# Fewer chunks for layer 1's queries and gates, planned buffer counts, and the last weighting shared by three engines

## The chip, the cores and the metric

The kernel runs on one core of a Trainium2 chip. The metric is the device time of one execution in microseconds (us). The engines are named as the profile names them: PE (TensorE, matmul), PEld (its weight load), DVE (VectorE), ACT (ScalarE), POOL (GpSimd) and SP (SyncE, which here issues transfers). A name with q behind it (ACTq, SPq) is that engine's sequencer, where transfers and waits on semaphores stand.

## The reference

Two layers work on 1040 tokens (16 meta tokens and 1024 real ones) of width 1024. The meta tokens fall away at the end, and a last RMS norm is applied.

```python
for layer in range(2):
    u = rms_norm(h, norm_g[layer])
    dq, dk, dv, dz, fq, fk, fv, fz, f_logit = split(u @ w_in[layer])
    # 4 "diff" heads: two rotated query/key pairs of 64 each, values of 128
    q1, q2 = rope(dq parts); k1, k2 = rope(dk parts)
    p = softmax(causal(q1 k1^T / 8)) - lam * softmax(causal(q2 k2^T / 8))
    o_a = rms_norm(p @ v_a, subln_g) * (1 - lambda_init)
    # 8 "fox" heads of 64: softmax with a cumulative forget bias, no rope
    p = softmax(causal(q_f k_f^T / 8 + cum_q - cum_k))
    o_b = p @ v_f
    h = h + concat(o_a * silu(dz), o_b * silu(fz)) @ w_out[layer]
return rms_norm(h, final_g)[16:]
```

## The kernel before

Every fp32 operand of a large matmul is split into a high and a low part, and a product of two such operands is three matmuls: high by high, low by high, high by low. The transposed, normed activations lie in SBUF as `XTh` and `XTl` (1024 channels as 8 groups of 128, by 1040 tokens). A projection of 128 output columns is `proj` (L344): for each chunk of tokens, 8 channel groups times 3 matmuls into one PSUM tile `pj`, as wide as the chunk. The chunks of a projection come from a list: layer 0 uses `CH_ALL`, or `CH_BLK` where the chunks have to end on token blocks. Layer 1's queries and gates are needed for the 1024 real tokens alone and use `CH_REAL` (L334), three chunks of 342, 342 and 340 columns. All keys use the full 1040 tokens in both layers.

A layer has eight units: 0 to 3 are the diff heads, 4 to 7 are pairs of fox heads. A unit is its projections of keys and queries (`unit_proj`, L482; the values of units 0 and 1 come from `proj_v01`, L384 to L423, whose matmul is L417), its attention (`attend`, L834), and its gate (`unit_gate`, L646). A layer ends with the out projection (matmul L1073), and per block of 128 tokens `out_half` (L1096 adds, L1097 squares) for each half of 512 channels and `out_close` (L1099).

For a diff unit, a chunk that PE has finished is copied by ACT (L502, tile `raw`), swapped by four transfers into `sw`, multiplied by cosine on DVE (L511) and by sine on POOL (L512), added on DVE (L513), and split into a high and a low part on ACT (L526) and DVE (L519). These steps run over groups of chunks: `RCH` is 2, so the three chunks of a query make a group of 684 columns and one of 340. Queries lie in the tiles `qa0`, `qa1` and `ql`, keys in `k0` and `k1`; a transfer on ACTq (L141) copies the high part to the other 64 partitions. Then come the scores (PE L690, L692, and L810, L811 for the meta tokens), the softmax on DVE (L696), ACT (L703) and POOL (L720), the transposes of the probabilities (PE L855, L865, L879), their split (ACT L773, DVE L774), and the products with the values (PE L795 to L800, L777 for the meta keys).

The program text doesn't fix the order on the engines. A scheduler with a planner's timeline (L1182) orders the instructions, and it also chooses how many buffers a tag has, wherever the kernel gives no number. `STB` = 3 gives a number to the tags `k0`, `k1`, `qa0`, `qa1` and `ql`. These tags hold more than keys and queries: at the start, the input blocks `hb` and the normed blocks `u` stand in them, and so does the raw weight of the first queries (`wraw4`, L306); at each layer's end, the split out weights `wo_k`, `wo_qa`, `wo_ql` do.

At the very end, `out_close` of the last token block works out the factor `r` of the norm on DVE, and then, for each half, `rms_apply` (L271) multiplies by `r` and by the gain `gb` in one DVE instruction, and SP issues the transfer out.

Of the kernel before, what the change touches and what calls it, by code (L numbers as in the profile page):

```python
# [16 lines left out]
AF = mybir.ActivationFunctionType  # L17
# [3 lines left out]
NM = 16  # L21
# [27 lines left out]
ENG = ('g','d')  # L49
WLB = 6  # L50
VPB = 0
STB = 3
NQZ = 3
PMB = 4
OTB = 2
# [58 lines left out]
def hybrid_kernel(ctx: ExitStack, tc: tile.TileContext, x, meta, norm_g, w_in, b_forget,  # L114
# [50 lines left out]

    small = [("es", 4, 272), ("ck", 2, 384), ("subn", 2, 36), ("sst", SSB, 8), ("ss", 3, 16), ("fn", 1, 64), ("fm", 1, 8), ("wf", 1, 64)]
    cst = const.tile([P, P + 96 + MW // 2 + sum(n * w for _, n, w in small)], F32, name="cst")
    rings, at = {}, P + 96 + MW // 2  # L170
    for nm, n, w in small:
# [159 lines left out]
        return his, los  # L331

    CH_ALL = [(0, 348), (348, 346), (694, 346)]
    CH_REAL = [(NM, 342), (NM + 342, 342), (NM + 684, 340)]  # L334
    CH_BLK = [(0, NM + 2 * P), (NM + 2 * P, 3 * P), (NM + 5 * P, 3 * P)]

    late = []
# [659 lines left out]
    for l in range(DEPTH):  # L997
# [101 lines left out]
        def out_close(opened):  # L1099

            b, hb, u, ss = opened
            t0, n = blk(b)
            if l == 0 and b > 0:
                dma(h1[t0:t0 + n], hb[:n])
            v, r = ss[:, 1, 0:1], ss[:, 2, 0:1]
            nc.vector.tensor_scalar(out=v[:n], in0=ss[:n, 0, 0:1], scalar1=1.0 / D, scalar2=EPS,
                                    op0=ALU.mult, op1=ALU.add)
            nc.vector.scalar_tensor_tensor(out=v[:n], in0=ss[:n, 0, 1:2], scalar=1.0 / D, in1=v[:n],
                                           op0=ALU.mult, op1=ALU.add)
            rsqrt(ss[:, 2], ss[:, 1], n, 1, ss[:, 3])  # L1110
            if l == 0:
                rms_apply(hb, n, r, gb, u)
                return lambda: put_ut(b, u)
            for hf in range(2):
                c = slice(512 * hf, 512 * hf + 512)
                rms_apply(hb[:, c], n, r, gb[:, c], u[:, c])
                dma(out2[P * (b - 1):P * b, c], u[:, c])
            return lambda: None

# [66 lines left out]
```

## Time and profile before

| what | value |
|---|---|
| median of 3 runs (lowest, highest) | 1485.57 us (1485.4, 1487.66) |
| the profiled execution's own time, its span | 1487.34 us, 1485.6 us |
| TensorE clock granted over the span | 0.983 of full |
| PE busy | 1416.9 us, 95% of the span |
| DVE, ACT, POOL busy | 958.7, 698.6, 619.2 us |
| chain of waits that ended last: PE, DVE, DMA | 75%, 7%, 4% of the span |

A busy share is the time in which an engine had an instruction running. The chain of waits follows the last instruction back, step by step, to what released it; its shares say which engine's work filled the time.

### The profile page before, as it was taken

What the parts mean: (1) busy time and instruction counts of PE and PEld (TensorE: products, weight loads), DVE (VectorE), ACT (ScalarE), POOL (GpSimd) and SP (SyncE); (2) the same over time, 40 slices, a digit from 0 to 9 for tenths busy, and PEclk for the clock granted to TensorE, in tenths of its full rate; (3) what the DMA queues carried; (4) which work ended last, traced back from release to release, by engine and by line L of the source; (5) the groups of instructions that cost most, each with busy time, mean ns of one, the idle gap of its engine ahead of it and who ended that gap; (6) DMA issues with size and microseconds to landing.
All of it is one profiled execution on the core that took longest, in us unless ns stands there. A gap on an engine that the chain in (4) does not pass through costs nothing.

```text
span 1485.6 us, 26706 instructions
## 1 busy us (share of the span) xinstructions
PE 1416.9 (95%) x9262; PEld 1350.0 (91%) x9262; DVE 958.7 (65%) x2721; ACT 698.6 (47%) x1729; POOL 619.2 (42%) x1118
## 2 busy tenths in 40 slices
PE   4889989999999999999998989999999999999997
PEld 4888989999999999996888989899999999999886
DVE  4548796867765666655654678677757565655554
ACT  3335554545554555554323455444446455544511
POOL 2616463542435443654015345445424444445400
PEclk7999999999999999999999999999999999999999
DMA  9315240353324234358333142324331323253632
GB/s 193 74 30 73 39 93 16 65 62 69 71 49 71 61 56 82 82 152 200 114 110 75 29 60 48 68 47 64 53 87 29 82 44 80 55 118 91 228 109 91
DMA packets 112215, 119.63 MB, mean 81 GB/s; under 512 B 15376, under 2 KB 92816, under 8 KB 112080
## 3 DMA queue, kind: packets, MB, share of 16 engines
q1 hardware_dynamic: 104592, 104.09, 32.2%
q10 hardware_dynamic: 7488, 13.83, 4.7%
q8 instruction: 73, 1.20, 0.3%
q14 instruction: 62, 0.51, 0.1%
HBM read 70.92 MB, written 21.54 MB: 62 GB/s over the span
## 4 chain that ended last, share of the span: by engine, by line
PE 75%; DVE 7%; DMA 4%; ACT 2%; issue 2%; SPq 1%; POOL 1%; DVEq 0%; ACTq 0%; POOLq 0%
PE pj L352 36%; PE pss L1073 5%; PE pj L1073 5%; PE pss L690 4%; PE pss L692 4%; PE pt L865 4%; PE po L800 3%; PE pj L417 3%; PE po L799 2%; DMA sw<-raw 1%; SPq L137 1%; DVE E L696 1%; PE pt L1073 1%; DVE raw L511 1%; DMA mt<-ms 1%
## 5 line engine op out<-in xcount | busy, mean ns | idle before, releaser
L352 PE MATMUL pj<-XTh,whi 128*128 128x346 f32 (+5 forms) x1392 | 453.8, 328 | 5.0 <-ACT XTh L296 1.9
L352 PE MATMUL pj<-XTh,wlo 128*128 128x346 f32 (+5 forms) x1392 | 452.9, 326 | 1.2 <-POOL wlo L328 1.2
L352 PE MATMUL pj<-XTl,whi 128*128 128x346 f32 (+5 forms) x1392 | 451.8, 325 | 1.1 <-DVE XTl L297 1.1
L352 PEld LDWEIGHTS pj<-XTh,whi 128*128 128x128 f32 x1392 | 264.3, 190 | 9.0 <-POOL whi L325 1.9
L352 PEld LDWEIGHTS pj<-XTh,wlo 128*128 128x128 f32 x1392 | 265.1, 190 | 2.5 <-POOL wlo L328 1.8
L352 PEld LDWEIGHTS pj<-XTl,whi 128*128 128x128 f32 x1392 | 264.8, 190 | 2.3 <-DVE XTl L297 1.7
L696 DVE CUSTOM_DVE_ANT_0 E<-pss,cst 128x346 f32<-128x346 f32 (+6 forms) x384 | 212.0, 558 | 77.0 <-PE pss L692 61.7
L703 ACT ACTIVATE E<-E,cst 128x656 f32<-128x656 f32 (+3 forms) x192 | 172.5, 898 | 141.7 <-DVE cst L696 137.8
L328 POOL TENSOR_TENSOR wlo<-wraw,whi 128x256 fp32r<-128x256 f32 x232 | 182.1, 785 | 16.3 <-PE pt L760 1.3
L774 DVE TENSOR_TENSOR ptl<-pt,pth 128x512 fp32r<-128x512 f32 (+1 forms) x240 | 147.6, 633 | 34.8 <-ACT pth L773 30.7
L690 PE MATMUL pss<-k,qa 128*128 128x400 f32 (+7 forms) x448 | 152.8, 347 | 12.1 <-DVE cst L696 6.9
L773 ACT CAST pth<-pt 128x512 fp32r<-128x512 f32 (+1 forms) x240 | 123.3, 545 | 72.8 <-PE pt L865 30.9
L325 POOL TENSOR_SCALAR whi<-wraw 128x256 fp32r<-128x256 f32 x232 | 101.0, 436 | 116.4 <-DMA wraw<-in_w_in_dram 115.2
L720 POOL TENSOR_SCALAR E<-E,cst 128x400 f32<-128x400 f32 (+2 forms) x96 | 83.7, 873 | 138.2 <-DVE cst L719 127.2
L673 POOL TENSOR_SCALAR XTl<-ql 64x128 fp32r<-64x128 f32 x136 | 53.0, 396 | 151.3 <-PE pss L692 127.3
L690 PEld LDWEIGHTS pss<-k,qa 128*128 128x128 f32 x448 | 84.8, 190 | 16.9 <-DVE cst L696 9.7
L865 PE MATMUL pt<-cst,E 128*128 128x128 f32 x576 | 87.1, 273 | 0.3 <-DVE cst L762 0.3
L799 PE MATMUL po<-pth,V 128*128 128x256 f32 x320 | 82.7, 283 | 0.0
L800 PE MATMUL po<-ptl,V 128*128 128x256 f32 x320 | 82.3, 286 | 0.0
L512 POOL TENSOR_TENSOR sw<-sw,sin 128x694 f32<-128x694 f32 (+5 forms) x32 | 50.6, 1581 | 76.0 <-DMA sw<-raw 63.8
L692 PE MATMUL pss<-k,q 68*128 68x400 f32 (+6 forms) x224 | 71.7, 326 | 0.5 <-DMA qa<-qa 0.5
L692 PE MATMUL pss<-k,XTl 128*128 128x400 f32 (+6 forms) x224 | 71.5, 325 | 0.0
(303 smaller groups left out, 2944.3 us busy)
## 6 DMA issues: line engine op xcount, KB each, us to landing
wraw<-in_w_in_dram SPq DMA_DIRECT2D x244, 128.0 KB
hb<-in_x_dram SPq DMA_DIRECT2D x16, 512.0 KB
wor<-in_w_out_dram SPq DMA_DIRECT2D x64, 128.0 KB
ms<-OT SPq DMA_DIRECT2D x8, 520.0 KB
k<-k ACTq DMA_DIRECT2D x16, 260.0 KB
h<-hb SPq DMA_DIRECT2D x8, 512.0 KB
ms<-OT SPq DMA_DIRECT2D x8, 512.0 KB
hb<-h SPq DMA_DIRECT2D x8, 512.0 KB
```

The lines of the kernel that those rows point to most:

```text
L328: nc.gpsimd.tensor_tensor(out=lo, in0=raw, in1=hi.bitcast(F32), op=ALU.subtract)
L352: nc.tensor.matmul(ps[:, :n], lhsT=w, rhs=xx[:, k, t0:t0 + n], start=(cnt == 0), stop=(cnt == 23))
L690: nc.tensor.matmul(ps[:, :nn], lhsT=U.Qa[m][:, t:t + P], rhs=U.K1[m][:, c0:c0 + nn], start=True, stop=False)
L692: nc.tensor.matmul(ps[:, :nn], lhsT=low[m], rhs=U.Kb[m][:, c0:c0 + nn], start=False, stop=True)
L696: nc.vector.tensor_tensor_reduce(out=E[:, c0:c0 + n], in0=ps[:, :n], in1=k, scale=-1.0, scalar=s[:, c - 1:c] if CHN and c else -NEG, op0=A ...
L703: nc.scalar.activation(E[:, :W], E[:, :W], AF.Exp, scale=-1.0, bias=lo, accum_out=s[:, 4:5])
L773: nc.scalar.copy(hi, ps)
L774: nc.vector.tensor_tensor(out=lo, in0=ps, in1=hi.bitcast(F32), op=ALU.subtract)
L799: nc.tensor.matmul(o[:, :256], lhsT=U.V[:, kb, hd, :], rhs=hi, start=False, stop=False)
L800: nc.tensor.matmul(o[:, :256], lhsT=U.V[:, kb, hd, :], rhs=lo, start=False, stop=last)
L865: nc.tensor.transpose(ps[:, (2 * a + b) * P:(2 * a + b + 1) * P], PP[:, k0:k0 + P], ident)
L1073: nc.tensor.matmul(ps, lhsT=xx[:, k, m0:m0 + P], rhs=wo[k][w][:, c], start=(k == 0 and i == 0), stop=(k == KT - 1 and i == 2))
```

## The change

There are four edits. `CH_REAL` becomes two chunks of 512 columns, for 16 projections of layer 1; with `RCH` = 2, both chunks of a query now make one group of 1024 columns. The ring `ck` in SBUF has slots of 512 instead of 384 columns, since a chunk of a fox query now needs them. `STB` becomes 0, so that the planner chooses the number of buffers for `k0`, `k1`, `qa0`, `qa1` and `ql`: it takes 2 of each. It also chooses anew for the tags that it planned before: the PSUM tag `pj` gets 3 instead of 2, `pss` 4 instead of 3; the others keep their numbers. And in the last block, half 0 is multiplied by the gain on POOL as soon as its sum is there (tile `hg`), and by `r` on ACT (L1118 of the changed kernel), while DVE does half 1.

```diff
--- before.py
+++ after.py
@@ -49,7 +49,7 @@
 ENG = ('g','d')
 WLB = 6
 VPB = 0
-STB = 3
+STB = 0
 NQZ = 3
 PMB = 4
 OTB = 2
@@ -165,7 +165,7 @@
 
 
 
-    small = [("es", 4, 272), ("ck", 2, 384), ("subn", 2, 36), ("sst", SSB, 8), ("ss", 3, 16), ("fn", 1, 64), ("fm", 1, 8), ("wf", 1, 64)]
+    small = [("es", 4, 272), ("ck", 2, 512), ("subn", 2, 36), ("sst", SSB, 8), ("ss", 3, 16), ("fn", 1, 64), ("fm", 1, 8), ("wf", 1, 64)]
     cst = const.tile([P, P + 96 + MW // 2 + sum(n * w for _, n, w in small)], F32, name="cst")
     rings, at = {}, P + 96 + MW // 2
     for nm, n, w in small:
@@ -331,7 +331,7 @@
         return his, los
 
     CH_ALL = [(0, 348), (348, 346), (694, 346)]
-    CH_REAL = [(NM, 342), (NM + 342, 342), (NM + 684, 340)]
+    CH_REAL = [(NM, 512), (NM + 512, 512)]
     CH_BLK = [(0, NM + 2 * P), (NM + 2 * P, 3 * P), (NM + 5 * P, 3 * P)]
 
     late = []
@@ -1113,7 +1113,11 @@
                 return lambda: put_ut(b, u)
             for hf in range(2):
                 c = slice(512 * hf, 512 * hf + 512)
-                rms_apply(hb[:, c], n, r, gb[:, c], u[:, c])
+                if b == NB and hf == 0:
+
+                    nc.scalar.activation(u[:, c], hg, AF.Copy, scale=r)
+                else:
+                    rms_apply(hb[:, c], n, r, gb[:, c], u[:, c])
                 dma(out2[P * (b - 1):P * b, c], u[:, c])
             return lambda: None
 
@@ -1127,6 +1131,7 @@
                 for hf in range(2):
                     out_mm(acc[b][hf], b, hf, k)
         todo = []
+        hg = None
         for b in first:
             ob = out_open(b)
             for hf in range(2):
@@ -1141,6 +1146,9 @@
                 for k in range(KT):
                     out_mm(ps2[hf], b, hf, k)
                 out_half(ob, ps2[hf], hf)
+                if l == 1 and b == NB and hf == 0:
+                    hg = st("hg")[:, :512]
+                    nc.gpsimd.tensor_tensor(out=hg, in0=ob[1][:, 0:512], in1=gb[:, 0:512], op=ALU.mult)
             for f in todo:
                 f()
             todo = [out_close(ob)]
```

PE has 384 matmuls fewer, DVE 33 instructions, ACT 26, POOL 11.

The order on the engines changes over the whole program, since the planner works with other counts. Three places show it. First, DVE at the start, where L271 makes the normed blocks: `u_242` to `u_244` are blocks 3 to 5, `u_304` to `u_306` are blocks 6 to 8, and L297 splits a transposed block. Before:

```order
L271 SCALAR_TENSOR_TENSOR u_242<-hb_167,cst_87,gb_142 128x1024
L271 SCALAR_TENSOR_TENSOR u_243<-hb_169,cst_87,gb_142 128x1024
L271 SCALAR_TENSOR_TENSOR u_244<-hb_171,cst_87,gb_142 128x1024
...
L271 SCALAR_TENSOR_TENSOR u_304<-hb_173,cst_87,gb_142 128x1024
L271 SCALAR_TENSOR_TENSOR u_305<-hb_175,cst_87,gb_142 128x1024
L271 SCALAR_TENSOR_TENSOR u_306<-hb_177,cst_87,gb_142 128x1024
L297 TENSOR_TENSOR XTl_97<-pt_260,XTh_96 128x4x128
```

After:

```order
L271 SCALAR_TENSOR_TENSOR u_304<-hb_173,cst_87,gb_142 128x1024
L271 SCALAR_TENSOR_TENSOR u_305<-hb_175,cst_87,gb_142 128x1024
L248 SCALAR_TENSOR_TENSOR cst_87<-cst_87 128x3
L271 SCALAR_TENSOR_TENSOR u_306<-hb_177,cst_87,gb_142 128x1024
...
L271 SCALAR_TENSOR_TENSOR u_242<-hb_167,cst_87,gb_142 128x1024
L271 SCALAR_TENSOR_TENSOR u_243<-hb_169,cst_87,gb_142 128x1024
L271 SCALAR_TENSOR_TENSOR u_244<-hb_171,cst_87,gb_142 128x1024
...
L297 TENSOR_TENSOR XTl_97<-pt_260,XTh_96 128x4x128
```

Blocks 6 to 8 are now normed ahead of blocks 3 to 5. On PE, the transposes keep the order of the blocks, 3 first.

Second, PE at the first scores of layer 0. L417 makes the values of units 0 and 1, 24 matmuls for each block of tokens (one name `pj_1024_...` each); L810 and what follows are scores. Before, they stand behind the second block of tokens, and one pair of L690 and L692 follows:

```order
L417 MATMUL pj_1024_703<-vwh,XTl 128x264
L810 MATMUL pss<-k_423,qa_527 128x16
L811 MATMUL pss<-k_423,XTl 128x16
L810 MATMUL pss<-k_424,qa_528 128x16
L811 MATMUL pss<-k_424,XTl 128x16
L690 MATMUL pss<-k_423,qa_527 128x400
L692 MATMUL pss<-k_423,XTl 128x400
L417 MATMUL pj_1024_733<-vwh,XTh 128x264
```

After:

```order
L417 MATMUL pj_1024_733<-vwh,XTl 128x264
L810 MATMUL pss<-k_423,qa_527 128x16
L811 MATMUL pss<-k_423,XTl 128x16
L810 MATMUL pss<-k_424,qa_528 128x16
L811 MATMUL pss<-k_424,XTl 128x16
L690 MATMUL pss<-k_423,qa_527 128x400
L692 MATMUL pss<-k_423,XTl 128x400
L690 MATMUL pss<-k_424,qa_528 128x400
L692 MATMUL pss<-k_424,XTl 128x400
L417 MATMUL pj_1024_763<-vwh,XTh 128x264
```

They now stand behind the third block's 24 matmuls, and two pairs of L690 and L692 stand there. In layer 1 the first scores moved likewise, from behind 48 of the matmuls of L417 to behind 96.

Third, DVE at the end of layer 1's attention. L789, L774 and L769 belong to attention, L1041 and L1053 to the out projection's operands (weights and gated outputs), L659 to a gate. Before:

```order
L789 TENSOR_TENSOR pm<-pt,pm 32x256
L774 TENSOR_TENSOR ptl<-pt,pth 128x512 x3
L659 SCALAR_TENSOR_TENSOR cst<-cst,pj_3840_17142 128x342
L774 TENSOR_TENSOR ptl<-pt,pth 128x384
L769 TENSOR_TENSOR OT<-po,otmp 64x256
L659 SCALAR_TENSOR_TENSOR cst<-cst,pj_3840_17170 128x340
L1053 TENSOR_TENSOR XTl<-mt,XTh 128x384 x3
L1041 TENSOR_TENSOR wo_k_17309<-wor,wo_k_17308 128x256 x2
L659 SCALAR_TENSOR_TENSOR cst<-cst,pj_3968_17223 128x342
L659 SCALAR_TENSOR_TENSOR cst<-cst,pj_3968_17251 128x342
L1041 TENSOR_TENSOR wo_k_17309<-wor,wo_k_17308 128x256 x2
L1053 TENSOR_TENSOR XTl<-mt,XTh 128x640 x2
```

After:

```order
L769 TENSOR_TENSOR OT<-po,otmp 64x256
L789 TENSOR_TENSOR pm<-pt,pm 32x256
L774 TENSOR_TENSOR ptl<-pt,pth 128x512 x2
...
L1053 TENSOR_TENSOR XTl<-mt,XTh 128x384
L1053 TENSOR_TENSOR XTl<-mt,XTh 128x640
L1041 TENSOR_TENSOR wo_ql<-wor,wo_qa_16884 128x256 x4
L774 TENSOR_TENSOR ptl<-pt,pth 128x512
L774 TENSOR_TENSOR ptl<-pt,pth 128x384
L1041 TENSOR_TENSOR wo_e<-wor,wo_e 128x256 x4
L769 TENSOR_TENSOR OT<-po,otmp 64x256
L1053 TENSOR_TENSOR XTl<-OT,XTh 128x640
```

The last attention's steps now stand among those of the out projection. On PE it is the same: before, no matmul of an out projection (L1073) stood ahead of its layer's last product with the values (L800), in either layer; now 83 rows of L1073 in layer 0 and 61 in layer 1 do.

How many matmuls stand on PE between the last one of a unit's query projection and the unit's first score, by the order:

| unit | 0 | 1 | 2 | 3 | 4 | 5 | 6 | 7 |
|---|---|---|---|---|---|---|---|---|
| layer 0 before | 68 | 142 | 144 | 141 | 97 | 118 | 99 | 117 |
| layer 0 after | 92 | 172 | 258 | 247 | 230 | 497 | 306 | 414 |
| layer 1 before | 64 | 42 | 70 | 64 | 32 | 43 | 94 | 76 |
| layer 1 after | 112 | 92 | 215 | 220 | 176 | 333 | 281 | 239 |

## Rows read from the trace of the kernel before

**Rows 1.** The page, part 1: busy us, share of span, instructions.

```profile
PE 1416.9 (95%) x9262; PEld 1350.0 (91%) x9262; DVE 958.7 (65%) x2721; ACT 698.6 (47%) x1729; POOL 619.2 (42%) x1118
```

**Rows 2.** Windows by stage: width, busy us (instructions) by engine, granted clock, DMA.

```profile
0.00:50.00 50.00, 25.48 (x146) 23.83 (x147) 25.21 (x66) 19.64 (x38) 21.85 (x44) 0.76 0.84 166
75.00:300.00 225.00, 209.12 (x1418) 200.98 (x1417) 170.24 (x486) 112.12 (x290) 105.32 (x185) 0.98 0.30 53
300.00:675.00 375.00, 374.99 (x2596) 367.46 (x2595) 245.18 (x739) 197.58 (x502) 168.81 (x327) 1.00 0.39 79
800.00:880.00 80.00, 70.49 (x477) 68.00 (x476) 57.16 (x158) 38.49 (x96) 30.84 (x55) 0.96 0.31 50
880.00:1040.00 160.00, 152.30 (x1031) 148.17 (x1030) 121.02 (x341) 79.47 (x198) 75.20 (x134) 0.98 0.29 53
```

**Rows 3.** Waits of PE: line, what for; total us, times, longest us.

```profile
PE pss L690 <- DVE cst L696: 6.9, 7, 2.0
PE po L777 <- DVE pm L789: 6.0, 4, 2.8
```

**Rows 4.** Timeline of PE, 342 columns in layer 1: start us, duration us, instruction.

```profile
1080.69 0.32 PE L352 MATMUL pj<-XTh,whi 128*128 128x342 f32 x1
...
1083.36 0.33 PE L352 MATMUL pj<-XTl,whi 128*128 128x342 f32 x1
```

**Rows 5.** Timeline of PE, 512 columns in the last out projection.

```profile
1473.82 0.39 PE L1073 MATMUL pss<-wo_ql,XTl 128*128 128x512 f32 x1
...
1475.45 0.40 PE L1073 MATMUL pss<-wo_ot,XTh 128*128 128x512 f32 x1
```

**Rows 6.** Timeline of PE, first scores of layer 0.

```profile
79.78 0.25 PE L810 MATMUL pss<-k,qa 128*128 128x16 f32 x1 [3.89 <-ACT V L421]
```

**Rows 7.** Timelines of PE, SPq, POOL, DVE, ACT, first scores of layer 1.

```profile
796.12 0.32 PE L352 MATMUL pj<-XTl,wroom 128*128 128x340 f32 x1
...
808.08 0.67 PE L690 MATMUL pss<-k,qa 128*128 128x400 f32 x1 [3.85 <-DMA qa<-qa]
796.16 4.95 SPq L137 DMA_DIRECT2D sw<-raw  x8
800.29 2.36 POOL L512 TENSOR_TENSOR sw<-sw,sin 128x684 f32<-128x684 f32 x1 [1.38 <-DMA sw<-raw]
803.71 0.87 DVE L513 TENSOR_TENSOR raw<-raw,sw 128x684 f32<-128x684 f32 x1
804.67 0.76 ACT L526 CAST qa<-raw 64x684 fp32r<-64x684 f32 x1 [1.93 <-DVE raw L513]
```

**Rows 8.** Timelines of DVE and PE, the start.

```profile
33.17 3.67 DVE L271 SCALAR_TENSOR_TENSOR u<-hb,cst,gb 128x1024 f32<-128x1024 f32 x3
...
38.43 3.81 DVE L271 SCALAR_TENSOR_TENSOR u<-hb,cst,gb 128x1024 f32<-128x1024 f32 x3
42.90 0.33 PE L286 MATMUL pt<-cst,u 128*128 128x128 f32 x1 [3.44 <-DVE XTl L297]
```

**Rows 9.** Timelines of DVE and ACT at the end; SP's transfers out (ns min/median/max).

```profile
1477.74 0.69 DVE L1096 TENSOR_TENSOR hb<-pss,hb 128x512 f32<-128x512 f32 x1 [3.89 <-PE pss L1073]
...
1481.00 1.42 DVE L271 SCALAR_TENSOR_TENSOR u<-hb,cst,gb 128x512 f32<-128x512 f32 x2
1478.46 0.63 ACT L1097 ACTIVATE u<-hb 128x512 f32<-128x512 f32 x1 [4.81 <-DVE hb L1096]
L137 SPq DMA_DIRECT2D out_dram<-u x16: 332/333/463, 1427.1 to 1482.4; - x16
```

**Rows 10.** Timelines of POOL and DVE, two rotary products that start together.

```profile
264.02 1.69 POOL L512 TENSOR_TENSOR sw<-sw,sin 128x694 f32<-128x694 f32 x1 [3.62 <-ACT sq L742]
264.19 2.25 DVE L511 TENSOR_TENSOR raw<-raw,cos 128x694 f32<-128x694 f32 x1
...
995.81 0.88 DVE L511 TENSOR_TENSOR raw<-raw,cos 128x694 f32<-128x694 f32 x1 [0.61 <-DMA sw<-raw]
995.85 2.38 POOL L512 TENSOR_TENSOR sw<-sw,sin 128x694 f32<-128x694 f32 x1 [10.91 <-DMA sw<-raw]
```

## The prediction

> **What bounds the kernel now.** I read the page's busy times first. PE is busy for 1416.9 of 1485.6 us, DVE for 958.7, ACT and POOL for less [rows 1]. So a gain comes from less matmul time, or from the 5% in which PE has nothing to do, or from what stands after PE's last matmul.
>
> Then I asked the windows where the 5% lie. From 300 to 675 us, the fox units, PE idles 0.01 us of 375 at full clock. From 75 to 300 us, the diff units of layer 0, it idles 225 − 209.1 = 15.9 us, and the granted clock is 0.98, which costs 0.02 × 225 = 4.5 more: 20.4. From 800 to 880 us it is 9.5 + 0.04 × 80 = 12.7, and from 880 to 1040 us 7.7 + 0.02 × 160 = 10.9. Together 44.0 us are lost in the diff units of the two layers. The first 50 us idle 24.5 [rows 2]. The reader is to see two kinds of stage: fox units, where PE is fed all the time and only fewer matmuls help, and diff units, where the order of the work decides.
>
> Next come the waits that end PE's idle time in the diff units. The longest two are 3.89 us ahead of the first scores of layer 0, put down to the values' copy on ACT [rows 6], and 3.85 us ahead of those of layer 1, for the transfer of the split queries [rows 7]. Waits for DVE's softmax and for the meta probabilities are 6.9 + 6.0 = 12.9 us over eleven places [rows 3].
>
> **Fewer chunks.** Twenty 342-column matmuls lie between 1080.69 and 1083.36 us with 17 steps between the two: 0.157 us each [rows 4]. Seven steps of 512 columns lie between 1473.82 and 1475.45: 0.233 each [rows 5]. A projection takes 24 × 3 × 0.157 = 11.3 us in three chunks (the 340 wide one, two columns less, makes it 0.04 less), and 24 × 2 × 0.233 = 11.2 in two. That is 0.08 a projection, and 1.3 for 16, all on PE and so on the path: **−1.3**. It is a small edit: the columns stay, and 384 matmuls go. DVE's and ACT's fewer instructions lie under PE and are worth nothing by themselves.
>
> **The last weighting.** After the last matmul, DVE adds (1477.74), ACT squares, DVE works out the factor, and two L271 take 1.42 us from 1481.00 [rows 9]. Now ACT does half 0 while DVE does half 1. The nearest row for ACT is its square of the same 128x512 at 0.63 us, so both halves are done after about 0.71, half of the 1.42. Both transfers then want SP at once, and the second waits for the first's issue, 0.33 by the median of sixteen [rows 9]: 0.71 − 0.33 makes **−0.4**, between 0 and −0.7. POOL's product with the gain has no row; L512's 694 columns took 1.69 alone, so 512 take about 1.25. It starts after the add of half 0, and DVE then sits idle for 3.89 us before 1477.74 [rows 9], with 3.3 more to 1481.0, so POOL's product is hidden. Without that cover it would cost up to 1.25.
>
> Here a shared port matters. Where POOL's L512 started first, at 264.02, it took 1.69 us, and DVE's L511, 0.17 later, 2.25; where DVE was first, at 995.81, DVE took 0.88 and POOL 2.38 [rows 10]. The first one keeps its speed and the other pays for both. That is the rule of the Trainium skill, "SBUF — State Buffer", section "SBUF: two separate sides": the port pair that DVE and GpSimd share is an exclusive lock, taken by whichever starts first, when the DVE operation has two SBUF inputs and the GpSimd one reads SBUF. The rule speaks against giving POOL a share of DVE's work: had its product run beside L271, the gain of 0.4 would turn to a loss of about 0.5 (1.25 less 0.71). The 3.89 us of idle DVE keep the two apart, so the sum is not changed.
>
> **The first scores.** In layer 0, 24 more value matmuls stand ahead of them. What PE waited for, 3.89 us, is mostly the same work done earlier or later, so the wait itself goes if 24 matmuls are enough. Those of L417 are 264 wide; from the 342 wide, an estimate is 264/342 × 0.157 = 0.121 each, so 24 are 2.9 us. Bounds 0 and −3.9; I take **−2.9**.
>
> In layer 1 the queries now come as one group of 1024 columns. Before, the query ended at 796.4, and the group of 684 was swapped from 796.16, when its buffer came free. Now: copy 0.6 (estimate), four issues at 0.6, landing 1.7 (796.16 + 2.4 to 800.29), POOL 2.36 × 1024/684 = 3.5, add 0.87 × 1.5 = 1.3, two casts 2 × 0.76 × 1.5 = 2.3, transfer and wait 1.9 (from 806.2, where the casts end, to 808.08). From 796.4 this ends at 810.1 [rows 7]. Before, 64 matmuls and 3.85 us of waiting filled the 11.7 us to 808.08; 48 more at 0.121 fill until about 796.4 + 7.8 + 5.8 = 810.0. The longer chain and the longer cover meet: I take **−3.5**, bounds 0 (the values' copies, which now stand on ACT ahead of the casts, hold it) and −3.9.
>
> **The other diff units.** The order puts 172 to 258 matmuls between query and scores where 142 to 144 stood in layer 0, and 92 to 220 where 42 to 70 stood in layer 1. Of the 44.0 us lost there, 7.7 are the two first waits and 12.9 are softmax and meta waits, which come from DVE's own pace. That leaves 23.4, waits for the chains of keys and queries and matmuls at half clock after a wait. More cover helps these; buffers reduced from three to two hold some back. I take two fifths, **−9**, between 0 and −23; the fraction is a choice, and the largest uncertainty.
>
> **What it costs.** At the start, blocks 3 to 5 are normed after blocks 6 to 8. Their L271 end at 38.43 + 3.81 = 42.2 instead of 33.17 + 3.67 = 36.8, and PE wants block 3 first: 5.4 us late, of which the 3.44 us that PE waited at 42.90 anyway may be got back [rows 8]. I take **+3**, between 2 and 5.4. At each layer's end, attention now stands within the out projection. What was run ahead as cover is no longer there to fill the last units' softmax; out-projection matmuls have to, and their weights wait for the buffers of the last keys and queries. Before, no wait of that kind is in the trace, so bounds are 0 and, if the last unit runs as the stretch 800 to 880 does now, 12.7 each. I take **+3** in layer 0 and **+2** in layer 1.
>
> **Sum.** −1.3 − 0.4 − 2.9 − 3.5 − 9 + 3 + 3 + 2 = −9.1. The profiled execution took 1487.34 us, with a span of 1485.6; it would be 1478.2. The median of the runs is 1.8 below that execution: 1485.57 − 9.1, about 1476.
>
> **The rivals.** First, stalls only move. The diff units' DVE is busy for 170.2 of 225 us already, and with softmax as the pace, each wait that goes is given back at the next. Then −9 and −2.9 fall away, the start and the ends stay, and −1.3 − 0.4 − 3.5 + 8 gives +2.8: about 1488; with start and ends at half of their 8, 1484. For it speak the 12.9 us for DVE; against it, that fox units follow, where PE never waits.
>
> Second, slower: the ends of the layers starve. Everything ahead goes as forecast, but the last units lack fillers, and each end loses the 12.7 us of the stretch 800 to 880. That is 25.4 instead of 5: 1476 + 20 = 1496. It decides from 15 us at the two ends together. Against it speaks that out-projection matmuls are many and depend on no one softmax; for it, that their operands (L1053, L1041) are made on the same DVE as the softmax.
>
> Third, the cover ends nearly all of the 23.4 us, and the ends cost nothing: 1476 − 14 − 5 = 1457.
>
> **How the numbers follow.** Forecast 0.45, from 1468 to 1482 by itself; first rival 0.23; second 0.2; third 0.12. A measurement of this kernel can tell about 0.2% or 3 us from no change. Faster than 1482.6: the forecast, the third rival, and little of the first: 0.6. Within: 0.18, most of the first. Slower than 1488.5: 0.22, the second and the upper part of the first. The range reaches into the second and third: 1461 to 1494.
>
> **What would show it.** In the changed profile: no wait over 1 us ahead of L810 at about 80 us or of L690 at about 810; from 75 to 300 and 800 to 1040 us, PE idle of about 22 in place of 33.1; the transposes L286 waiting for L271 near 38 to 42 us; waits of L1073, L799 or L690 within the out projections of under 3 us each; DVE with one L271 at the end. Wrong would make it: new waits of L690 for the 1024-wide query chain, DVE waits of over 7 us at a layer's end, or waits of L352 for the weight splits on POOL.

## The result: slower by 0.7%

Ten runs of the changed kernel have a median of 1499.45 us (1494.13 to 1504.21), ten of the kernel before 1489.24 us (1483.5 to 1493.53). The ratio is 1.007, with a 95% interval from 1.0047 to 1.0093. The median of the three runs that stood ahead of the prediction, 1485.57 us, is 3.7 us under the median of all ten; on its scale the result is 1485.57 × 1.007 = 1496.0. The profiled execution took 1500.85 us with a span of 1499.1, so the two profiled executions are 1500.85 − 1487.34 = 13.5 us apart.

The page's busy times and its chain by engine, of the changed kernel:

```profile
PE 1424.7 (95%) x8878; PEld 1317.0 (88%) x8878; DVE 957.5 (64%) x2688; ACT 695.4 (46%) x1702; POOL 618.4 (41%) x1107
PE 79%; DMA 6%; DVE 6%; issue 3%; POOL 3%; ACT 2%; SPq 1%; ACTq 0%; DVEq 0%; POOLq 0%
```

PE is busy for a little longer, 1424.7 instead of 1416.9 us [rows 1], though it has 384 matmuls fewer. The waits of PE (us in total, times, longest) say where it stood still:

```profile
PE pt L286 <- DVE u L271: 20.0, 3, 16.1
PE pj L1068 <- POOL wo_ot L1041: 4.2, 1, 4.2
PE po L777 <- DVE pm L789: 3.9, 4, 2.6
PE pss L690 <- DVE cst L696: 3.8, 4, 2.8
PE pss L690 <- DMA qa<-qa: 2.9, 1, 2.9
```

The 3.89 us ahead of layer 0's first scores [rows 6] are gone; the waits for softmax and meta probabilities are 3.8 and 3.9 instead of 6.9 and 6.0 [rows 3], and 2.8 of the 3.8 is one wait at the end of layer 0. New is a wait of 4.2 us in the out projection.

Where the time went is read best by the steps of the program. I cut each trace at four events: the first score; the first product with the values of a fox unit (L800); layer 1's first value matmul (L417); layer 1's first product of a fox unit. For each stage I summed how much later each matmul started than the columns of the one before it need; one that started sooner counts against the sum. That need is 0.457 ns a column, from [rows 4, 5], and at least 0.11 us, the step of the 128 column transposes (L865) where nothing holds them. This loss takes in waits and slow clock together. The windows of the changed kernel at these events (columns as in [rows 2]):

```profile
0.00:82.00 82.00, 55.99 (x349) 54.56 (x349) 44.46 (x92) 31.06 (x63) 41.70 (x66) 0.83 0.62 129
82.00:426.00 344.00, 330.50 (x2208) 317.42 (x2207) 237.57 (x701) 160.72 (x425) 146.97 (x268) 0.99 0.34 57
426.00:821.00 395.00, 381.86 (x2357) 348.61 (x2357) 237.83 (x675) 182.69 (x453) 157.40 (x284) 0.99 0.40 93
821.00:1156.00 335.00, 322.12 (x2014) 298.46 (x2013) 230.30 (x628) 157.09 (x376) 142.04 (x259) 0.98 0.36 58
1156.00:1414.00 258.00, 257.07 (x1629) 236.05 (x1628) 171.23 (x481) 149.00 (x349) 121.99 (x223) 1.00 0.39 93
```

From 426 to 821 us, layer 0's fox units and its end, PE idles 395 − 381.9 = 13.1 us. In the kernel before, PE idled 0.01 us from 300 to 675 [rows 2], and 1.9 in the whole stage, from 398 to 798. The loss by stage, in us:

| stage | before | changed | difference |
|---|---|---|---|
| start, to the first score | 34.3 | 33.1 | −1.2 |
| diff units of layer 0 | 22.0 | 26.8 | +4.8 |
| fox units and end of layer 0 | 4.8 | 23.7 | +18.9 |
| diff units of layer 1 | 28.6 | 20.5 | −8.1 |
| fox units and end of layer 1 | 3.4 | 2.3 | −1.1 |
| sum | 93.1 | 106.4 | +13.3 |

So the gain in layer 1's diff units is there, and layer 0 eats it, in a stage that was nearly without loss. By the same count, some 16.6 of layer 0's 23.7 us fall between 650 and 725 us, its end, where the kernel before loses 1.8; the fox units ahead of it lose some 7 instead of 3. At the end of layer 0, PE shows this:

```profile
669.67 0.75 PE L690 MATMUL pss<-k,qa 128*128 128x456 f32 x1 [2.79 <-DVE cst L696]
...
680.67 0.50 PE L1073 MATMUL pss<-wo_qa,XTh 128*128 128x512 f32 x1 [1.20 <-POOL wo_qa L1041]
...
717.32 0.66 PE L1068 MATMUL pj<-wo_ot,mm 128*48 128x512 f32 x1 [4.20 <-POOL wo_ot L1041]
```

The wait of 2.79 us is for DVE, whose rows ahead of it are these:

```profile
665.38 0.54 DVE L696 CUSTOM_DVE_ANT_0 E<-pss,cst 128x328 f32<-128x328 f32 x1
665.86 0.08 DVE L696 DVE_READ_ACCUMULATOR2_ANT cst<- 128x1 f32 x1
665.86 1.30 DVE L1053 TENSOR_TENSOR XTl<-mt,XTh 128x400 fp32r<-128x400 f32 x2
667.08 0.41 DVE L1041 TENSOR_TENSOR wo_k<-wor,wo_ql 128x256 fp32r<-128x256 f32 x1
668.55 0.58 DVE L1053 TENSOR_TENSOR XTl<-mt,XTh 128x400 fp32r<-128x400 f32 x1 [1.06 <-ACT XTh L1052]
669.04 0.56 DVE L696 CUSTOM_DVE_ANT_0 E<-pss,cst 128x392 f32<-128x392 f32 x1
```

Between two steps of the softmax (L696) stand three splits of gated outputs and one of an out weight (L1053, L1041), and the third of the former waited 1.06 us for ACT. The softmax went on 3.1 us after the step before it had ended, and PE waited for it: here it is the order on DVE that costs.

POOL shows this:

```profile
708.25 0.41 POOL L325 TENSOR_SCALAR whi<-wraw 128x256 fp32r<-128x256 f32 x1 [3.94 <-DMA wraw<-in_w_in_dram]
...
709.43 0.80 POOL L661 TENSOR_TENSOR OT<-OT,cst 128x346 f32<-128x346 f32 x1
714.46 0.40 POOL L325 TENSOR_SCALAR whi<-wraw 128x256 fp32r<-128x256 f32 x1 [4.23 <-DMA wraw<-in_w_in_dram]
715.87 0.72 POOL L1041 TENSOR_TENSOR wo_ot<-wor,wo_ot 128x256 fp32r<-128x256 f32 x1 [1.00 <-DMA ms<-OT]
```

The wait of 4.20 us is for `wo_ot`, an out weight that POOL splits (L1041). Its buffer is the one in which the last unit's gated output stood, and POOL did that product (L661) only at 709.43, behind a split of layer 1's weights (L325) that had waited 3.94 us for its transfer. The last row of attention's output in that buffer (DVE L769, 705.73 to 706.16) had been ready 3.3 us before. Behind the product came the transfer of the output (`ms<-OT`), issued at 710.26, and L1041 waited until that had landed and began at 715.87. A second such split at 714.46 had waited 4.23 us, but was done before that. Around the two waits, the windows 667 to 681 and 712 to 725 us show the idle time and the clock:

```profile
667.00:681.00 14.00, 9.12 (x31) 6.90 (x32) 11.44 (x32) 10.38 (x26) 5.48 (x8) 0.76 0.84 248
712.00:725.00 13.00, 8.80 (x32) 5.89 (x31) 1.64 (x2) 0.58 (x1) 5.03 (x8) 0.87 0.69 86
```

In the first, PE idles 4.9 of 14 us, and the granted clock is 0.76; in the second it idles 4.2 of 13, at 0.87. So for part of the time the matmuls behind the waits run at the lower of the clock's two levels (1.2 GHz), which is worth 0.24 × 14 + 0.13 × 13 = 5.1 us. With the idle time that is 14.2 of the 16.6 us of layer 0's end. In the kernel before, layer 0's attention was over when its out projection began.

### The profile page after: what moved, and what is told of

Same layout as the page of the kernel before. It is cut to its first block, busy times and chain, and to the rows that moved or that the text cites. A ratio compares the mean times of both kernels' runs of the same rounds, so it can differ in the third digit from the quotient of the medians.

```text
span 1499.1 us, 25917 instructions
## 1 busy us (share of the span) xinstructions
PE 1424.7 (95%) x8878; PEld 1317.0 (88%) x8878; DVE 957.5 (64%) x2688; ACT 695.4 (46%) x1702; POOL 618.4 (41%) x1107
## 3 DMA queue, kind: packets, MB, share of 16 engines
q1 hardware_dynamic: 103824, 104.09, 33.1%
## 4 chain that ended last, share of the span: by engine, by line
PE 79%; DMA 6%; DVE 6%; issue 3%; POOL 3%; ACT 2%; SPq 1%; ACTq 0%; DVEq 0%; POOLq 0%
PE pj L352 39%; PE pss L1073 5%; PE pj L1073 5%; PE pss L690 4%; PE pss L692 4%; PE pt L865 3%; DMA wraw<-in_w_in_dram 3%; PE pj L417 2%; PE po L799 2%; PE po L800 2%; PE po L797 1%; PE po L795 1%; PE po L796 1%; DVE E L696 1%; PE pt L1073 1%
## 5 line engine op out<-in xcount | busy, mean ns | idle before, releaser
L352 PE MATMUL pj<-XTh,whi 128*128 128x346 f32 (+4 forms) x1272 | 433.5, 343 | 14.0 <-POOL whi L325 3.2
L352 PE MATMUL pj<-XTh,wlo 128*128 128x346 f32 (+4 forms) x1272 | 432.7, 341 | 0.9 <-POOL wlo L328 0.8
L352 PE MATMUL pj<-XTl,whi 128*128 128x346 f32 (+4 forms) x1272 | 431.5, 340 | 0.9 <-DVE XTl L297 0.9
L352 PEld LDWEIGHTS pj<-XTh,whi 128*128 128x128 f32 x1272 | 241.1, 190 | 28.4 <-POOL whi L325 3.7
L696 DVE CUSTOM_DVE_ANT_0 E<-pss,cst 128x456 f32<-128x456 f32 (+6 forms) x384 | 211.9, 558 | 70.9 <-PE pss L692 42.4
L352 PEld LDWEIGHTS pj<-XTh,wlo 128*128 128x128 f32 x1272 | 242.3, 191 | 10.6 <-POOL wlo L328 2.2
L352 PEld LDWEIGHTS pj<-XTl,whi 128*128 128x128 f32 x1272 | 242.0, 190 | 10.2 <-DVE XTl L297 1.1
L703 ACT ACTIVATE E<-E,cst 128x400 f32<-128x400 f32 (+2 forms) x192 | 172.4, 898 | 141.8 <-DVE cst L696 135.9
L328 POOL TENSOR_TENSOR wlo<-wraw,whi 128x256 fp32r<-128x256 f32 x232 | 177.1, 764 | 52.1 <-PE pj L352 38.1
L325 POOL TENSOR_SCALAR whi<-wraw 128x256 fp32r<-128x256 f32 x232 | 104.6, 451 | 227.6 <-DMA wraw<-in_w_in_dram 169.3
L774 DVE TENSOR_TENSOR ptl<-pt,pth 128x512 fp32r<-128x512 f32 (+1 forms) x240 | 148.3, 633 | 51.2 <-ACT pth L773 40.4
L690 PE MATMUL pss<-k,qa 128*128 128x400 f32 (+7 forms) x448 | 151.1, 341 | 8.1 <-DVE cst L696 3.8
L690 PEld LDWEIGHTS pss<-k,qa 128*128 128x128 f32 x448 | 85.0, 190 | 14.7 <-DVE cst L696 5.9
L865 PE MATMUL pt<-cst,E 128*128 128x128 f32 x576 | 83.6, 273 | 1.4 <-DVE cst L762 1.2
L800 PE MATMUL po<-ptl,V 128*128 128x256 f32 x320 | 83.0, 288 | 0.5 <-POOL ptl L885 0.5
L692 PE MATMUL pss<-k,q 68*128 68x400 f32 (+6 forms) x224 | 72.8, 328 | 0.0
L865 PEld LDWEIGHTS pt<-cst,E 128*128 128x128 f32 x576 | 67.9, 141 | 4.1 <-DVE cst L762 1.5
L692 PE MATMUL pss<-k,XTl 128*128 128x400 f32 (+6 forms) x224 | 70.9, 321 | 0.0
```

The costliest lines, as they stand in the source:

```text
L328: nc.gpsimd.tensor_tensor(out=lo, in0=raw, in1=hi.bitcast(F32), op=ALU.subtract)
L352: nc.tensor.matmul(ps[:, :n], lhsT=w, rhs=xx[:, k, t0:t0 + n], start=(cnt == 0), stop=(cnt == 23))
L690: nc.tensor.matmul(ps[:, :nn], lhsT=U.Qa[m][:, t:t + P], rhs=U.K1[m][:, c0:c0 + nn], start=True, stop=False)
L692: nc.tensor.matmul(ps[:, :nn], lhsT=low[m], rhs=U.Kb[m][:, c0:c0 + nn], start=False, stop=True)
L696: nc.vector.tensor_tensor_reduce(out=E[:, c0:c0 + n], in0=ps[:, :n], in1=k, scale=-1.0, scalar=s[:, c - 1:c] if CHN and c else -NEG, op0=A ...
L703: nc.scalar.activation(E[:, :W], E[:, :W], AF.Exp, scale=-1.0, bias=lo, accum_out=s[:, 4:5])
```

## The experiments

Each is a whole kernel, timed in five rounds against the kernel before on the same chip. The ratio is of runs to runs of before, with its 95% interval. Loss by stage is worked out as above from one profile each. The kernel before and e1 have the same order but for the last block, and their losses differ by 5.0 us in layer 0's diff units and 1.6 at the start, so smaller differences are not read.

| kernel | ratio (interval) | start | diff 0 | fox 0, end | diff 1 | fox 1, end | out matmuls early | fox steps 0 |
|---|---|---|---|---|---|---|---|---|
| before | 1 | 34.3 | 22.0 | 4.8 | 28.6 | 3.4 | 0 | 98, 119, 100, 118 |
| e1 | 0.9999 (0.9977, 1.0020) | 35.9 | 27.0 | 4.4 | 28.8 | 3.3 | 0 | as before |
| e4 | 1.0028 (1.0006, 1.0050) | 37.4 | 23.6 | 4.6 | 29.7 | 5.6 | 0 | as before |
| e5 | 0.9969 (0.9954, 0.9983) | 36.8 | 20.7 | 4.9 | 23.0 | 1.5 | 0 | as before |
| e9 | 0.9968 (0.9954, 0.9982) | 37.3 | 26.4 | 5.2 | 21.1 | 1.2 | 0 | as before |
| e12 | 0.9973 (0.9956, 0.9990) | 37.5 | 24.7 | 5.3 | 25.1 | 1.1 | 0 | as before |
| e6 | 1.0007 (0.9992, 1.0023) | 39.1 | 24.6 | 6.1 | 24.1 | 1.2 | 6 | 98, 119, 97, 136 |
| e11 | 1.0013 (0.9995, 1.0032) | 31.9 | 27.0 | 4.2 | 26.8 | 2.1 | 14 | 100, 252, 173, 228 |
| e7 | 1.0005 (0.9990, 1.0019) | 34.6 | 22.5 | 17.4 | 17.2 | 3.0 | 67 | 251, 351, 285, 405 |
| e3 | 1.0092 (1.0057, 1.0126) | 37.7 | 29.9 | 11.5 | 24.7 | 2.6 | 54 | 88, 212, 172, 200 |
| changed | 1.0070 (1.0047, 1.0093) | 33.1 | 26.8 | 23.7 | 20.5 | 2.3 | 84 | 231, 498, 307, 415 |
| e2 | 1.0125 (1.0089, 1.0161) | 34.1 | 24.3 | 19.8 | 21.9 | 11.0 | 0 | 98, 74, 57, 57 |
| e8 | 1.0195 (1.0170, 1.0220) | 33.5 | 28.1 | 23.9 | 26.1 | 12.7 | 0 | 98, 74, 57, 57 |
| e10 | 1.0239 (1.0213, 1.0264) | 33.1 | 31.9 | 27.6 | 29.5 | 10.5 | 0 | 130, 76, 56, 52 |

The last two columns are of the order in layer 0: how many matmuls of the out projection stand ahead of the last product with the values, and how many steps stand on PE from a fox unit's queries to its scores (units 4 to 7, counted with both ends).

**e1, the last weighting alone.** `CH_REAL`, `ck` and `STB` as before, the rest of the change kept.

```diff
-STB = 0
+STB = 3
-    CH_REAL = [(NM, 512), (NM + 512, 512)]
+    CH_REAL = [(NM, 342), (NM + 342, 342), (NM + 684, 340)]
```

> The last weighting alone: three chunks, three buffers each, the order elsewhere as before. All theories: the same time as before within 0.2%. The DVE instruction of half 0 goes from the end, ACT does it beside DVE, and the time from the last matmul's sum to the last transfer's issue falls by 0.3 to 0.7 us. If GpSimd's product collided with DVE's work, the end would be about 0.5 us longer instead.

Measured 0.9999 (0.9977 to 1.0020): no difference, as expected. The time from the last sum to the end of the last transfer's issue fell by 0.13 us, from 5.04 to 4.91, where 0.3 to 0.7 was expected.

**e2, the change with before's PSUM counts.** `PSB` gives the numbers of PSUM tiles for `pj`, `pss`, `pt` and `po`; with 0 the planner chooses. In the changed kernel:

```diff
-PSB = (0, 0, 0, 0)
+PSB = (2, 3, 4, 1)
```

> The whole change, with the PSUM counts of before written down (2 for pj, 3 for pss, 4 for pt, 1 for po) instead of 3 and 4 chosen by the planner. Theory A: the loss of the change comes from the order in layer 0, where with more PSUM tiles projections run ahead, and the last unit's attention and gate end within the out projection. Here no matmul of an out projection stands ahead of its layer's last product with the values, so the 25 us lost from 300 to 725 us go, the gains in the diff units of layer 1 stay in part, and it is faster than before by 3 to 12 us. Theory B: two buffers instead of three for keys, queries and out weights are the cause; they are two here too, so 10 us or more of the loss stay and it is slower than before or the same. Theory C: the 1024 wide query group in layer 1 costs; then layer 1 loses time from 800 to 1040 us.

Measured 1.0125 (1.0089 to 1.0161). Theory A, as put here, fell: no out matmul stands early, and layer 0's fox units and end lose 19.8 us all the same, layer 1's 11.0. Theory B was left standing.

**e3, two buffers alone.** In the kernel before:

```diff
-STB = 3
+STB = 0
```

> The buffer counts alone left to the planner: three chunks and the end as before, 2 buffers each for keys and queries, PSUM 2 for pj and 3 for pss, 3 for pt. In its order 54 of layer 0's out matmuls stand ahead of the last product with the values (84 in the changed kernel, 0 before), none in layer 1. Theory A: a loss at the end of layer 0, smaller than in the changed kernel, 5 to 12 us from 300 to 725 us, and little or no gain in the diff units. Theory B: 10 us or more, spread over both layers, also at layer 1's end. Theory C: as before.

Measured 1.0092 (1.0057 to 1.0126): slower, with 11.5 us in layer 0's fox units and end. Neither the two chunks nor the last weighting are in this kernel, so they aren't needed for the loss. Theory C can't explain it. It is the size that theory A expected; of theory B's loss at layer 1's end there is nothing (2.6 us, 3.4 before).

**e4, queries alone in two chunks.** In the kernel before, in `unit_proj`:

```diff
-        ch_q = (CH_BLK if j in CKB else CH_ALL) if l == 0 else CH_REAL
+        ch_q = (CH_BLK if j in CKB else CH_ALL) if l == 0 else [(NM, 512), (NM + 512, 512)]
```

> Only layer 1's queries in two chunks of 512: the gates keep three, three buffers each, PSUM counts and layer 0's order as before, the end as before. In layer 1, 89, 115, 95, 90 matmuls stand between the queries and the first scores of the diff units, where 65, 43, 71, 65 stood. Theory A: layer 0 takes the time of before, and layer 1's diff units lose 5 to 12 us less: 1474 to 1482 on the scale of 1485.6. Theory C: the 1024 wide chain holds the scores, waits of L690 for the query transfer of 2 us or more in units 0 to 3, and the time is that of before or longer.

Measured 1.0028 (1.0006 to 1.0050). Layer 0 is as before, but the gain of 5 to 12 us in layer 1's diff units isn't there: 29.7 us of loss. Part of theory C held: PE waited 8.4 us, in five places, for query transfers of layer 1, 6.1 of them in one.

**e5, the change with three key buffers and two query buffers.** In the changed kernel, with a look-up of the tag's count in `Sized.tile`:

```diff
-STB = 0
+STB = 0; TB = {'k0': 3, 'k1': 3, 'qa0': 2, 'qa1': 2, 'ql': 2}
-        n = int(np.prod(shape[1:]))
+        n = int(np.prod(shape[1:])); bufs = TB.get(tag or name, bufs)
```

> The whole change, with three buffers for the key tags k0 and k1 and two for qa0, qa1 and ql. The planner then takes 2 for pj and 3 for pss, and its order in layer 0 has before's counts (69, 143, 145, 142, 98, 119, 100, 118 steps from a unit's queries to its scores, no out matmul ahead of the last product with the values). Theory D, the order costs: layer 0 loses from the first fox product to layer 1's values the 5 us or so of before instead of 24, and the time is 0.994 to 1.003 of before. Theory B, two buffers for queries or out weights cost by themselves: 10 us or more of loss in layer 0's fox units and its end, slower by 0.5% or more.

Measured 0.9969 (0.9954 to 0.9983), faster than both kernels. The window of layer 0's fox units and end in its profile:

```profile
399.00:800.00 401.00, 399.09 (x2516) 370.03 (x2515) 240.79 (x676) 185.27 (x463) 165.76 (x297) 1.00 0.42 97
```

PE idles 1.9 of 401 us. Theory D, the order costs, comes in here with its forecast. It held, and theory B is wrong for queries: two buffers of `qa0`, `qa1` and `ql` cost nothing there, once the order is that of before. The whole change is in this kernel, all of its chunks and the new end.

**e6, the same with two key buffers and three query buffers.** `TB` with 2 for the keys and 3 for the others.

> The whole change, with two buffers for k0 and k1 and three for qa0, qa1 and ql. Layer 0's order is that of before but for the last two units (97, 136) and 6 out matmuls ahead of the last product. Theory D: 0.994 to 1.004 of before, layer 0 as before within 4 us. Theory B, two key buffers cost: 10 us or more in layer 0's fox units and end.

Measured 1.0007 (0.9992 to 1.0023), layer 0's fox units and end 6.1 us. Two key buffers cost at most a little by themselves. What e3 and the changed kernel lose isn't the count of either group alone.

**e7, e6's counts without the change.** In the kernel before, the same `TB`.

> The kernel before (three chunks, old end) with two buffers for k0 and k1 and three for qa0, qa1 and ql. Here the planner takes 4 for pj, and its order runs far ahead: 251, 351, 285, 405 steps from queries to scores in layer 0's fox units, 67 out matmuls ahead of the last product. Theory D: like the changed kernel, 10 to 20 us lost in layer 0's fox units and end, 5 to 10 us gained in the diff units, 1.003 to 1.009 of before. Theory C, the two chunks of 512 cost: the time of before or shorter.

Measured 1.0005 (0.9990 to 1.0019), below the expected 1.003 to 1.009. The two sides of theory D are both in it: 17.4 us lost in layer 0's fox units and end, 12.6 more than before, and layer 1's diff units at 17.2 instead of 28.6, a gain of 11.4. They cancel. The waits of PE that are longest from 423 to 812 us:

```profile
PE pt L856 <- POOL E L720: 3.3, 1, 3.3
PE pj L352 <- DVE OT L769: 1.3, 1, 1.3
```

**e8, two buffers each with before's PSUM counts.** In the kernel before:

```diff
-STB = 3
+STB = 2
-PSB = (0, 0, 0, 0)
+PSB = (2, 3, 4, 1)
```

> The kernel before with two buffers of each of the five tags and its own PSUM counts written down. Its order in layer 0 is that of the experiment with PSUM fixed: 74, 57, 57 steps from queries to scores in units 5 to 7, where before had 119, 100, 118; no out matmul ahead of the last product. Theory D: 10 to 15 us more lost in layer 0's fox units and end, as in that experiment, and 3 to 8 us in layer 1's fox units: 1.006 to 1.013 of before. Theory C: the time of before, since there are three chunks.

Measured 1.0195 (1.0170 to 1.0220), more than expected. It has e2's order in layer 0, with few steps between the last units' queries and scores, and loses there as e2 does, 23.9 and 19.8 us. Waits of PE from 398 to 823 us:

```profile
PE pss L1073 <- ACT wo_k L1040: 4.0, 2, 3.1
PE pt L856 <- POOL E L720: 3.9, 2, 2.6
```

L856 waits for POOL's share of the softmax, and the out projection for ACT's cast of its weights.

**e9, e5 with each chunk by itself.** In `project`, in e5:

```diff
-                if t0 + n < L and len(todo) < RCH:
+                if t0 + n < L and len(todo) < (RCH if l == 0 else 1):
```

> The change with three key and two query buffers (0.997 of before), and in layer 1 each chunk of 512 columns turned and split by itself instead of both as one group of 1024. Layer 0's order is that of before. If the 1024 wide chain is what PE waits for at layer 1's first scores (5.8 us there), that wait falls to 3 us or less and the time to 0.992 to 0.996 of before, faster than either kernel. If the wait is for the last part of the queries whatever its width, or the values' copies, it stays at 4 us or more, and twice as many small transfers and products on DVE and POOL bring 0.997 to 1.000.

Measured 0.9968 (0.9954 to 0.9982), the same as e5. The first wait of layer 1 fell from 5.8 to 3.5 us, between the two expectations (3 us or less, 4 or more), and the gain that was expected with it didn't come.

**e10, e5 with the changed kernel's PSUM counts.** In e5:

```diff
-PSB = (0, 0, 0, 0)
+PSB = (3, 4, 4, 1)
```

> The change with three key and two query buffers, and the PSUM counts of the changed kernel (3 for pj, 4 for pss). Its order has the changed kernel's long run-ahead in layer 0's diff units (93, 173, 293, 258 steps from queries to scores), but little in its fox units (130, 76, 56, 52), and no out matmul ahead of the last product. Theory D, the order costs: layer 0's fox units and end lose 10 us or more again, as in the two kernels with 74, 57, 57; 1.004 to 1.012 of before, though no buffer is fewer than in the kernel with 0.997. If PSUM counts don't matter beyond the order of layer 0's end, 0.995 to 1.000.

Measured 1.0239 (1.0213 to 1.0264), the slowest of all, 2.7% over e5 with the same matmuls, chunks and key and query buffers, and twice the upper bound of what was expected. About half of the 27.6 us in layer 0's fox units and end falls between 600 and 650 us, where PE waits 3.83 us once for softmax and the granted clock is 0.90; much of the rest is in small waits, such as the first three of these:

```profile
491.94 0.39 PE L690 MATMUL pss<-k,qa 128*128 128x264 f32 x1 [0.22 <-DVE cst L696]
...
493.01 0.36 PE L690 MATMUL pss<-k,qa 128*128 128x272 f32 x1 [0.22 <-DVE k L519]
...
496.89 0.33 PE L879 MATMUL pt<-cst,E 128*128 128x128 f32 x1 [0.26 <-DVE ptl L774]
...
628.56 0.45 PE L855 MATMUL pt<-cst,E 128*96 128x128 f32 x1 [3.83 <-DVE cst L719]
```

**e11, the change with three buffers each.** In the changed kernel:

```diff
-STB = 0
+STB = 3
-("ck", 2, 512)
+("ck", 1, 512)
```

> The whole change with three buffers of all five tags; to fit, the gates' ring has one slot of 512 columns instead of two. The planner takes 3 for pj and 4 for pss. Layer 0's order: 93, 153, 101, 91 in the diff units, 100, 252, 173, 228 in the fox units, 14 out matmuls ahead of the last product (0 before, 84 in the changed kernel). Theory D: a loss between, 4 to 12 us in layer 0's fox units and end, 0.998 to 1.006 of before. Theory B, two buffers are what costs: layer 0 as before, 0.993 to 0.998. One gate slot may add waits of GpSimd and ScalarE at the gates, off the path of PE.

Measured 1.0013 (0.9995 to 1.0032). The PSUM counts are those of e10 and of the changed kernel, and layer 0's fox units and end lose 4.2 us, as in the kernel before. So PSUM counts of 3 and 4 aren't the cause by themselves either. A kernel with two gate slots and three buffers each wasn't tried.

**e12, e5 with only the gates in two chunks.** In e5, `unit_proj` with the three chunks of before:

```diff
-        ch_q = (CH_BLK if j in CKB else CH_ALL) if l == 0 else CH_REAL
+        ch_q = (CH_BLK if j in CKB else CH_ALL) if l == 0 else [(NM, 342), (NM + 342, 342), (NM + 684, 340)]
```

> The change with three key and two query buffers, but only the gates in two chunks of 512; the queries keep three. Layer 0's order is that of before. If the two chunks are worth the 0.08 us a projection that the matmuls save, 0.6 us here, 0.998 to 1.001 of before; if the gain of the 0.997 comes from the order in layer 1's diff units, which here have 65, 89, 93, 65 steps instead of 89, 91, 112, 90, about half of it is seen, 0.997 to 1.000.

Measured 0.9973 (0.9956 to 0.9990), nearly all of e5's gain with three chunks for the queries. Two query buffers and the new end are in it too, so it doesn't say that the gates bring the gain.

**What follows.** Theories A, B and C each have a kernel against them: e2 and e11 against PSUM counts, e5 and e6 against buffer counts, e3 and e5 against the chunks. Each of them is against one cause by itself. Theory D stays, and the DVE rows at 665 us show one place where the order costs; but the counts set the order in every kernel, so that two counts together cost something beside it is not excluded. No kernel has the same counts in another order. In layer 0's fox units and end, the kernels with before's order or near it lose 4 to 6 us; those with some 50 to 76 steps in the last units lose 20 to 28; those in which 54 and more out matmuls stand early lose 11 to 24. Of kernels with 0, 6, 14, 54, 67 and 84 early out matmuls (and at least 88 steps), the losses are 4.8, 6.1, 4.2, 11.5, 17.4 and 23.7. The long run-ahead by itself seems not to cost: e11 has 252, 173 and 228 steps in the last units with 14 early out matmuls and loses 4.2 us, e3 has 212, 172 and 200 with 54 and loses 11.5. But e11 also has three buffers where e3 has two, so this is argued, not shown. Open is also why so small a change of a count moves the whole order. (The early matmuls are counted in the traces; for the changed kernel that gives 84 in layer 0 and 54 in layer 1, where the section on the change has 83 and 61.)

## Why the prediction was wrong

**The step that failed** is the one on what the change costs: +3 at layer 0's end, and nothing in its fox units. The two measured +18.9 together, some 15 of it at the end and 4 in the fox units. The mechanism named there, the last attention within the out projection, is what the trace shows, but the price was bounded by 12.7 us, a stretch of diff units, and taken near zero. Part of the price is what the second rival named, operands of the out projection on DVE ahead of the softmax: the wait of 2.79 us. Part was left out, what else stands at layer 0's end on POOL: the split of layer 1's weights, which waits for its transfer and holds the last gate, the transfer of its output and the out weights behind it: the wait of 4.20 us. And the slower clock behind the two added 5.1 us. At layer 1's end, where no next layer's weights come, +2 was forecast and −1.1 came. So the second rival was right in layer 0 and wrong in layer 1, and it got a chance of 0.2. That its 1496 is also what was measured on the scale of the first runs is luck: it had 12.7 us at each end, and all gains as forecast.

**Fewer chunks, −1.3.** Too small to be seen by itself, and not sure as a sum either: starts are shown to 0.01 us, which over 17 steps and 72 matmuls is 0.04 us of the 0.08 a projection, and over 7 steps and 48 matmuls 0.07. (The two columns less of the third chunk are 24 × 2 × 0.457 ns = 0.02 us, not 0.04.) e12 and e5 gain about 0.3% or 4 us, more than the matmuls give; their profiles have 25.1 and 23.0 us in layer 1's diff units instead of 28.6. Queries alone (e4) gave nothing. Whether the gates' chunks bring the 4 us or the two query buffers, which e5, e9 and e12 share, is open. One sentence of the section on the change was wrong: the 512 column slots of `ck` serve the gates (`unit_gate`), not the fox queries.

**The last weighting, −0.4.** At the end of the program it measured 0.0 by the profiles; the ratio of e1 can't tell 0.4 us from none. DVE, then ACT, POOL and SP at the end of the changed kernel:

```profile
1491.23 0.69 DVE L1096 TENSOR_TENSOR hb<-pss,hb 128x512 f32<-128x512 f32 x1 [3.63 <-PE pss L1073]
...
1494.50 0.75 DVE L271 SCALAR_TENSOR_TENSOR u<-hb,cst,gb 128x512 f32<-128x512 f32 x1
```

```profile
1494.58 0.72 ACT L1118 ACTIVATE u<-hg,cst 128x512 f32<-128x512 f32 x1 [1.91 <-DVE cst L248]
1487.00 1.29 POOL L1151 TENSOR_TENSOR hg<-hb,gb 128x512 f32<-128x512 f32 x1 [61.86 <-DMA out_dram<-u]
1495.33 0.81 SPq L137 DMA_DIRECT2D out_dram<-u  x2
```

POOL's product took 1.29 us for an estimate of 1.25 and was hidden, and ACT's half took 0.72 beside DVE's 0.75, as forecast. But the second transfer's issue ended at 1496.14, 4.91 us after the last add began, and before it was 5.04. The forecast took 0.33 for the first issue, by which the second waits; here the two back to back took 0.81. The end of the span lies 1499.1 − 1491.23 = 7.87 us after that add; in the kernel before 1485.6 − 1477.74 = 7.86 [rows 9].

**First scores.** In layer 0 the wait is gone, and the start costs about what was forecast. The blocks 3 to 5 are normed last, as these rows of DVE, and then one of PE, show.

```profile
35.61 2.62 DVE L271 SCALAR_TENSOR_TENSOR u<-hb,cst,gb 128x1024 f32<-128x1024 f32 x2
...
38.43 1.84 DVE L271 SCALAR_TENSOR_TENSOR u<-hb,cst,gb 128x1024 f32<-128x1024 f32 x1
...
41.30 3.82 DVE L271 SCALAR_TENSOR_TENSOR u<-hb,cst,gb 128x1024 f32<-128x1024 f32 x3
...
42.73 0.66 PE L286 MATMUL pt<-cst,u 128*128 128x128 f32 x2 [3.76 <-DVE u L271]
```

They end at 45.1 us, 8.3 later than the 36.8 of [rows 8]; 5.4 was forecast. Until the first score the loss is 1.2 us less than before; the wait of 3.9 and the start together make that, so the start cost about 2.7 where +3 was forecast (two profiles of one order differ by 1.6 there).

In layer 1, −3.5 was forecast, and the wait went from 3.85 to 2.90:

```profile
835.62 0.42 PE L690 MATMUL pss<-k,qa 128*128 128x400 f32 x1 [2.90 <-DMA qa<-qa]
```

That is one of the signs of being wrong that the prediction named: over 1 us, for the 1024 wide query chain. In e5, with less cover, it is 5.83. Its rows on PE, ACT, SP and POOL show which part of the chain was wrong:

```profile
797.43 0.39 PE L352 MATMUL pj<-XTl,wroom 128*128 128x512 f32 x1
...
814.35 0.67 PE L690 MATMUL pss<-k,qa 128*128 128x400 f32 x1 [5.83 <-DMA qa<-qa]
```

```profile
799.33 1.05 ACT L526 CAST k<-raw 64x384 fp32r<-64x384 f32 x2 [6.43 <-DVE raw L513]
800.41 0.60 ACT L502 ACTIVATE raw<-pj 128x512 f32<-128x512 f32 x1
...
810.13 1.04 ACT L526 CAST qa<-raw 64x1024 fp32r<-64x1024 f32 x1 [2.89 <-DVE raw L513]
```

```profile
801.03 2.41 SPq L137 DMA_DIRECT2D sw<-raw  x4
805.34 3.44 POOL L512 TENSOR_TENSOR sw<-sw,sin 128x1024 f32<-128x1024 f32 x1 [4.07 <-DMA sw<-raw]
```

Swap 2.41, POOL 3.44 and casts 2.11 us are near the estimates (2.4, 3.5, 2.3). But the query ended at 797.8, and ACT copied its second chunk at 800.41: the casts of the keys, queued ahead of it, had waited for DVE's L513. The forecast let the copy begin as soon as PE was done.

**The other diff units, −9.** Layer 1 gained 8.1 with its first scores, whose wait fell by 0.95, so about 7 here. Layer 0 gained nothing that can be told from the 5 us by which two profiles of one order differ.

**The range** of 1461 to 1494 didn't hold the median of 1499.45, nor 1496.0 on the scale of the first runs: the 12.7 us that bounded an end were too few for layer 0, and the fox units had no term.

## What to carry to other kernels

Where a planner sets both order and buffer counts, a change in one count is a change of the whole program: here the same work ran from 0.997 to 1.024. Look at the order of the stages in which the engine never waited, since they have only time to lose, and pin the counts so that their order stays while the edit is tried. A gain from more work run ahead as cover has to be set against the place from which that cover was taken.

## What the runs showed of the hardware

Idle time understates what short waits cost. In e10, PE idles 420 − 408.2 = 11.8 us from 410 to 830 us, and the stage's loss is 27.6. A 342 column matmul is shown for 0.32 us while the next may start 0.157 later [rows 4], so a step can be 0.16 us late with no idle time to see; only the starts show it. Of the 15.8 us between the two numbers, some 5 are the granted clock, 0.90 from 600 to 650 us; the rest is such lateness. The granted clock fell behind waits of a few us: it was 0.76 and 0.87 in the two windows at layer 0's end, with waits of 2.79 and 4.20 us in them, and 1.00 from 398 to 798 us in the kernel before. And ten runs of the kernel before spread over 0.7%, from 1483.5 to 1493.53 us.
